# A layer of attention and RWKV-7: softmax exponentials placed further behind their scores in a hand-made plan

## The chip, the core and the metric

The kernel runs on one core of one Trainium2 chip. The metric is device time in microseconds. Five engines matter: PE (TensorE, the matrix engine), DVE (VectorE), ACT (ScalarE), POOL (GpSimd) and SP (SyncE, which issues DMAs). Each works through its own queue in order; a tile passes from one to another through semaphores.

## What is computed

One decoder layer over 2048 tokens of width 1024, in float32. After an RMS norm, one projection feeds two groups of heads side by side: eight attention heads with two key-value heads, and eight RWKV-7 heads. Their outputs share one output projection; then come a gated feed-forward part with a causal convolution and a last RMS norm. The change touches the attention heads alone. Cut to what matters there:

```python
def sliding_window_attention(q, k, v, sinks):
    # per block of 128 queries: its own 128 keys and the 128 before them
    s = jnp.einsum('bnqkgd,bnskd->bnkgqs', qb, kb) * (HEAD_DIM ** -0.5)
    s = s - slopes[:, :, None, None] * dist.astype(f32)
    s = jnp.where(valid[None, :, None, None], s, NEG_INF)
    m = jnp.maximum(jnp.max(s, axis=-1, keepdims=True), sink)
    p = jnp.exp(s - m)
    denom = jnp.sum(p, axis=-1, keepdims=True) + jnp.exp(sink - m)
    o = jnp.einsum('bnkgqs,bnskd->bnqkgd', p / denom, vb)
```

The RWKV-7 heads run a recurrence over the tokens, `S_t = S_(t-1) (diag(w_t) - kk_t^T (a_t kk_t)) + v_t^T k_t`, `y_t = S_t r_t`; the kernel computes it in chunks.

## The kernel before

**Two stages.** Up to about 1212 us the kernel projects, attends and runs the recurrence; after that come the rest of the output projection and the feed-forward part, which the change doesn't touch. The first stage is cut into 16 units: four blocks `b` of 512 tokens by four pairs `j` of heads. A unit (b, j) is named so below. The names of its tiles end in `_b_j_...`.

**What a unit holds.** Its backbone is a chain of eight chunks of the recurrence: PE products into `pc` and `pY`, and between them evictions by ACT: `Pt`, `Ut`, `SV`. Each chunk needs the one before, so between its products PE has gaps ("hops", 24 in a unit), which are filled with two kinds of work. The dense pieces are matmuls of the input projection for a later unit (`pin_q`, `pin_r`, ...). The placed pieces have a position from 0 to 24 in the unit, from the table `Q` at the top of the file (L43 to L80), and are issued when the chain has come so far. Among them are the attention of the unit before, the output of the recurrence (`py`, `pg`), a triangular substitution on DVE (`Mt`, `M`, 31 steps, one step woven in behind each other DVE instruction), and the loading and transposing of the next block's input (`ht`).

**The attention of a unit** comes in four quarters (q2, g): two halves of the block's queries, two key-value heads. A quarter has three placed pieces, with a row of four positions each in `Q["at0"]` to `Q["at3"]`, one table for each pair:

- scores (L1006): products into `pS` on PE; DVE adds the bias and takes the maximum (`P<-pS`), then writes the negated maximum and one more small operand, both into the tile `m`.
- transposes (`ptr`, L1054): PE transposes the normalised P into `pT`; ACT copies it rounded (`pth`), DVE takes the rest (`ptl`).
- value products (`pv`, L1070): twelve products into `pO`, evicted by ACT to `oT`.

`pS`, `pT` and `pO` share one PSUM pool with two buffers, the P tiles a pool with two as well.

**What is deferred.** Between scores and transposes lie two more steps. They are not placed by position: a planner's clock, which counts microseconds of planned work (L396 to L411), runs them later. `go1` (L1038) puts the exponentials of the sink and of the scores on ACT, due `Q["p1"]` after the scores. `go2` (L1045) adds the sums, takes the reciprocal and normalises P, all on DVE, due `Q["p2"]` after `go1`. If they are still to do when the transposes are issued, `need` runs them first:

```python
def tick(us):
    clk["t"] += us
    while todo and todo[0][0] <= clk["t"]:
        todo.pop(0)[2]()
```

All of PE, ACT and DVE are issued through `in_order` (L94), which ties each instruction to the one before it on its engine. So the plan is the order of the queues: an instruction whose operand is late holds all that stand behind it on its engine.

Of the kernel before, what the change touches and what calls it, by code (L numbers as in the profile page):

```python
# [54 lines left out]
    "y2": 1.5,  # L55
    "ql": 1.0,
    "p2": 1.2,
    "p1": 1.8,
    "tl": 0.8,
    "hop": 0.25,  # L60
    "sub": (6.5, 17.0, 21.0, 22.0, 23),
# [1787 lines left out]
```

## Time and profile before

| | |
|---|---|
| median of three runs | 2682.79 us (2681.02 to 2684.7) |
| profiled execution | 2685.55 us |
| its span | 2683.8 us |
| PE busy | 2534.4 us, 94% of the span |
| DVE, ACT, POOL busy | 1740.1, 1285.3, 1469.0 us |

The profiled execution is 2.76 us over the median. Busy time of PE is an upper view, since matmuls are pipelined and their ends are modelled. An instruction's row in the timeline gives its start, its length, engine and line, what it writes and reads, and in brackets how long the engine stood idle before it and which instruction on which engine released it.

### The profile page before, as it was taken

What the parts mean: (1) busy time and instruction counts of PE and PEld (TensorE: products, weight loads), DVE (VectorE), ACT (ScalarE), POOL (GpSimd) and SP (SyncE); (2) the same over time, 40 slices, a digit from 0 to 9 for tenths busy, and PEclk for the clock granted to TensorE, in tenths of its full rate; (3) what the DMA queues carried; (4) which work ended last, traced back from release to release, by engine and by line L of the source; (5) the groups of instructions that cost most, each with busy time, mean ns of one, the idle gap of its engine ahead of it and who ended that gap; (6) DMA issues with size and microseconds to landing.
All of it is one profiled execution on the core that took longest, in us unless ns stands there. A gap on an engine that the chain in (4) does not pass through costs nothing.

```text
span 2683.8 us, 42227 instructions
## 1 busy us (share of the span) xinstructions
PE 2534.4 (94%) x15211; PEld 1988.0 (74%) x15211; DVE 1740.1 (65%) x3232; ACT 1285.3 (48%) x2753; POOL 1469.0 (55%) x1364
## 2 busy tenths in 40 slices
PE   7799999999999989998989999999999999999997
PEld 5566766767667666776768788787888888888886
DVE  6568776777677757644756777867676765453336
ACT  4356655665556555543434434345343343343343
POOL 6334443444444434321637777777666665564598
PEclk9899998999999989899979999999999999999999
DMA  4222222222223222335662444545233326742354
GB/s 126 62 70 74 74 71 74 66 68 76 70 59 96 64 66 74 80 116 182 189 203 86 157 141 144 161 162 192 83 110 102 118 91 233 237 158 102 102 166 172
DMA packets 333108, 313.94 MB, mean 117 GB/s; under 512 B 102576, under 2 KB 254274, under 8 KB 332898
## 3 DMA queue, kind: packets, MB, share of 16 engines
q1 hardware_dynamic: 332290, 310.71, 38.1%
q8 instruction: 119, 1.95, 0.3%
q14 instruction: 91, 0.75, 0.1%
q10 hardware_dynamic: 608, 0.53, 0.1%
HBM read 229.26 MB, written 81.92 MB: 116 GB/s over the span
## 4 chain that ended last, share of the span: by engine, by line
PE 62%; DVE 17%; DMA 7%; ACT 5%; issue 4%; POOL 4%; SPq 0%; POOLq 0%; ACTq 0%; DVEq 0%
PE q_g L104 14%; PE d L104 14%; PE q_u L104 13%; DVE M L124 4%; DVE Mt L124 4%; PE pin_q L104 3%; PE poa L104 3%; DMA LL<-dL 3%; PE px L104 2%; PE po L104 2%; PE pc L104 2%; DVE P L124 2%; PE pin_k L104 1%; PE ph L104 1%; PE pO L104 1%
## 5 line engine op out<-in xcount | busy, mean ns | idle before, releaser
L1262 POOL TENSOR_TENSOR ul_u<-s_u,uh_u 128x512 fp32r<-128x512 f32 x154 | 214.4, 1401 | 138.0 <-ACT uh_u L110 134.8
L1262 POOL TENSOR_TENSOR ul_a<-sa,uh_a 128x512 fp32r<-128x512 f32 x154 | 210.9, 1377 | 139.7 <-ACT uh_a L110 139.7
L1262 POOL TENSOR_TENSOR ul_g<-s_g,uh_g 128x512 fp32r<-128x512 f32 x154 | 220.9, 1442 | 60.9 <-ACT uh_g L110 54.8
L104 PE MATMUL q_g<-h2h,uh_g 128*128 128x512 f32 x616 | 242.6, 394 | 10.0 <-DVE u_g L1486 5.9
L104 PE MATMUL q_g<-h2l,uh_g 128*128 128x512 f32 x616 | 241.7, 392 | 0.0
L104 PE MATMUL q_g<-h2h,ul_g 128*128 128x512 f32 x616 | 241.5, 393 | 0.1
L104 PE MATMUL q_u<-h2h,uh_u 128*128 128x512 f32 x616 | 240.2, 390 | 1.3 <-DVE ct L1486 1.0
L104 PE MATMUL q_u<-h2h,ul_u 128*128 128x512 f32 x616 | 239.9, 389 | 0.9 <-POOL ul_u L1262 0.9
L104 PE MATMUL q_u<-h2l,uh_u 128*128 128x512 f32 x616 | 239.7, 389 | 0.0
L104 PE MATMUL d<-ul_b,uh_a 128*128 128x512 f32 x616 | 232.9, 390 | 1.8 <-DVE ul_b L1483 1.8
L104 PE MATMUL d<-uh_b,ul_a 128*128 128x512 f32 x616 | 229.5, 389 | 0.0
L110 ACT ACTIVATE uh_a<-sa 128x512 fp32r<-128x512 f32 x154 | 97.1, 631 | 229.1 <-PE d L104 122.3
L104 PE MATMUL d<-uh_b,uh_a 128*128 128x512 f32 x616 | 205.9, 389 | 0.0
L110 ACT ACTIVATE uh_u<-s_u 128x512 fp32r<-128x512 f32 x154 | 95.1, 628 | 223.5 <-DVE s_u L1483 113.8
L124 DVE TENSOR_TENSOR Mt<-M,LL 128x60 f32<-128x60 f32 (+24 forms) x496 | 159.2, 321 | 41.7 <-DMA LL<-dL 33.3
L110 ACT ACTIVATE uh_g<-s_g 128x512 fp32r<-128x512 f32 x154 | 95.3, 629 | 186.3 <-PE q_u L104 102.7
L1483 DVE TENSOR_TENSOR ul_b<-wd,uh_b 128x512 fp32r<-128x512 f32 x55 | 68.6, 1249 | 156.1 <-ACT uh_b L110 150.1
L124 DVE SCALAR_TENSOR_TENSOR cc<-g,fcst,cc 128x1024 f32<-128x1024 f32 x88 | 145.4, 1670 | 29.1 <-ACT cc L110 28.4
L124 DVE TENSOR_TENSOR M<-M,Mt 128x60 f32<-128x60 f32 (+24 forms) x496 | 155.7, 314 | 10.8
L104 PEld LDWEIGHTS q_g<-h2h,uh_g 128*128 128x128 f32 x616 | 117.0, 190 | 36.0 <-DVE u_g L1486 7.2
L104 PEld LDWEIGHTS d<-ul_b,uh_a 128*128 128x128 f32 x616 | 115.6, 188 | 27.8 <-DVE ul_b L1483 4.1
L104 PEld LDWEIGHTS q_u<-h2h,uh_u 128*128 128x128 f32 x616 | 115.6, 188 | 27.2 <-DVE ct L1486 1.4
(371 smaller groups left out, 7017.5 us busy)
## 6 DMA issues: line engine op xcount, KB each, us to landing
sa<-actc SPq DMA_DIRECT2D x77, 512.0 KB
s_g<-in_ffn_w_gate_dram SPq DMA_DIRECT2D x44, 512.0 KB
s_u<-in_ffn_w_up_dram SPq DMA_DIRECT2D x44, 512.0 KB
actc<-cc SPq DMA_DIRECT2D x88, 256.0 KB
actc<-sa SPq DMA_DIRECT2D x66, 256.0 KB
wd<-in_ffn_w_down_dram SPq DMA_DIRECT2D x22, 512.0 KB
s_cat<-catT SPq DMA_DIRECT2D x20, 512.0 KB
x<-in_x_dram SPq DMA_DIRECT2D x16, 512.0 KB
```

The costliest lines, as they stand in the source:

```text
L104: in_order("pe", nc.tensor.matmul(**kw))
L110: in_order("act", nc.scalar.activation(*args, **kw))
L124: in_order("dve", f(*args, **kw))
L1262: return nc.gpsimd.tensor_tensor(out=out, in0=in0, in1=in1, op=ALU.subtract)
L1483: return nc.vector.tensor_tensor(out=out, in0=in0, in1=in1, op=ALU.subtract)
```

## The change

Two entries of the table change; no instruction is added or removed.

```diff
--- before.py
+++ after.py
@@ -55,7 +55,7 @@
     "y2": 1.5,
     "ql": 1.0,
     "p2": 1.2,
-    "p1": 1.8,
+    "p1": 4.0,
     "tl": 0.8,
     "hop": 0.25,
     "sub": (6.5, 17.0, 21.0, 22.0, 23),
@@ -69,7 +69,7 @@
     "py": (10, 10, 11),
     "vt": 1,
     "xl": (4, 14, 16, 23.6),
-    "at0": ((6.5, 9, 17.5, 18.5), (9.5, 13.5, 20, 20.0), (13, 16, 20.5, 22)),
+    "at0": ((6.5, 9, 16.5, 18.0), (10.5, 13.5, 20, 21.5), (13, 16, 21, 23)),
     "at1": ((4.5, 6, 13.5, 15.5), (8, 12.5, 18.5, 21.5), (10, 17.5, 20.5, 23)),
     "at2": ((4.5, 6, 13.5, 17.0), (9, 13, 18, 21), (11.0, 14, 20, 23)),
     "at3": ((4, 6, 10, 14), (8.5, 11.5, 16.5, 19.5), (10.5, 13.5, 19.5, 23.6)),
```

`p1` puts the exponentials, and with them the normalisation, later behind their scores by the planner's clock: 4.0 us in place of 1.8. It holds for all units. In `at0`, the table of the first pair of each block, the third and fourth scores come earlier (17.5 to 16.5, 18.5 to 18.0), the first and fourth transposes later (9.5 to 10.5, 20.0 to 21.5), and so do the third and fourth value products (20.5 to 21, 22 to 23).

In the built program PE's order changes in the four units of pair 0 alone. On ACT and DVE the exponentials and normalisations of all pairs move.

Unit (1, 1), ACT: `m` and `P` are the exponentials of the third quarter, `Pt` and `Ut` the evictions of chunk 5, `sh_v3` and `carry` belong to the input of a later unit. Before:

```order
L110 ACTIVATE SV_1_1_4512<-pc_1_1_4_5800,eC2_134 64x64 x2
L110 ACTIVATE m_1_1_1_0_5856<-m_1_1_1_0_5856 128x2
L110 ACTIVATE P_1_1_1_0_5855,m_1_1_1_0_5856<-P_1_1_1_0_5855,m_1_1_1_0_5856 128x256 x2
L110 ACTIVATE Pt_1_1_5_5898<-pc_1_1_5_5897 128x64
L110 ACTIVATE sh_v3_1_5958<-pin_v3_1_5793,omu_118 128x512
L110 ACTIVATE carry_119<-pin_v3_1_5793 128x1
L110 ACTIVATE Ut_1_1_5_5899<-pc_1_1_5_5897 128x64
```

After:

```order
L110 ACTIVATE SV_1_1_4512<-pc_1_1_4_5800,eC2_134 64x64 x2
L110 ACTIVATE Pt_1_1_5_5895<-pc_1_1_5_5894 128x64
L110 ACTIVATE m_1_1_1_0_5856<-m_1_1_1_0_5856 128x2
L110 ACTIVATE P_1_1_1_0_5855,m_1_1_1_0_5856<-P_1_1_1_0_5855,m_1_1_1_0_5856 128x256 x2
L110 ACTIVATE sh_v3_1_5950<-pin_v3_1_5793,omu_118 128x512
L110 ACTIVATE carry_119<-pin_v3_1_5793 128x1
L110 ACTIVATE Ut_1_1_5_5896<-pc_1_1_5_5894 128x64
```

The first eviction of the chunk now stands ahead of the exponentials.

The same unit, DVE: the last steps of the substitution (`M`, `Mt`) with the normalisation of the third quarter (`m` twice, `P` twice) between them; `hr` and `v` are pieces of later inputs. Before:

```order
L124 RECIPROCAL m_1_1_1_0_5856<-m_1_1_1_0_5856 128x2
L124 TENSOR_TENSOR Mt_1_2_30_5946<-M_1_2_5491,LL_1_2_5490 128x8
L124 TENSOR_SCALAR P_1_1_1_0_5855<-P_1_1_1_0_5855,m_1_1_1_0_5856 128x256
L124 TENSOR_TENSOR M_1_2_5491<-M_1_2_5491,Mt_1_2_30_5946 128x8
L124 TENSOR_SCALAR P_1_1_1_0_5855<-P_1_1_1_0_5855,m_1_1_1_0_5856 128x256
L124 TENSOR_TENSOR hr_2_2_3351<-pth_11_1_5967,cst0_107 128x2x128
L124 TENSOR_TENSOR hr_2_3_3352<-pth_11_1_5967,cst0_107 128x2x128
L124 SCALAR_TENSOR_TENSOR v_1_3_5957<-pin_v3_1_5793,cst1_108,sh_v3_1_5958 128x511
L124 SCALAR_TENSOR_TENSOR v_1_3_5957<-carry_119,cst1_108,sh_v3_1_5958 128x1
L124 TENSOR_TENSOR m_1_1_1_1_5914<-m_1_1_1_1_5914 128x2
```

After:

```order
L124 TENSOR_TENSOR hr_2_2_3348<-pth_11_1_5956,cst0_107 128x2x128
L124 TENSOR_TENSOR M_1_2_5491<-M_1_2_5491,Mt_1_2_29_5933 128x8x2
L124 TENSOR_TENSOR hr_2_3_3349<-pth_11_1_5956,cst0_107 128x2x128
L124 TENSOR_TENSOR Mt_1_2_30_5964<-M_1_2_5491,LL_1_2_5490 128x8
L124 SCALAR_TENSOR_TENSOR v_1_3_5949<-pin_v3_1_5793,cst1_108,sh_v3_1_5950 128x511
L124 TENSOR_TENSOR M_1_2_5491<-M_1_2_5491,Mt_1_2_30_5964 128x8
L124 SCALAR_TENSOR_TENSOR v_1_3_5949<-carry_119,cst1_108,sh_v3_1_5950 128x1
L124 TENSOR_TENSOR m_1_1_1_0_5856<-m_1_1_1_0_5856 128x2
L124 RECIPROCAL m_1_1_1_0_5856<-m_1_1_1_0_5856 128x2
L124 TENSOR_SCALAR P_1_1_1_0_5855<-P_1_1_1_0_5855,m_1_1_1_0_5856 128x256 x2
```

The normalisation now stands behind two `hr` and two `v`.

Unit (1, 0), PE, near its end: `pT_1_0_1_1` are the fourth transposes, `pO_1_0_1_0` the third value products, `pc_1_0_7` the products of the last chunk, `pin_q1` the dense work. Before:

```order
L104 MATMUL pin_q1_1_5212<-hh_1_3_2702,wh_q1_1_5062 128x512
L104 MATMUL pin_q1_1_5212<-hl_1_3_2703,wh_q1_1_5062 128x512
L104 MATMUL pin_q1_1_5212<-hh_1_3_2702,wl_q1_1_5063 128x512
L107 MATMUL pT_1_0_1_1_5244<-ident_64,P_1_0_1_1_5156 128x128 x4
L104 MATMUL pO_1_0_1_0_5252<-pth_1_0_1_0_5230,vth_130 64x128
L104 MATMUL pO_1_0_1_0_5252<-ptl_1_0_1_0_5231,vth_130 64x128
L104 MATMUL pO_1_0_1_0_5252<-pth_1_0_1_0_5230,vtl_131 64x128
```

After:

```order
L104 MATMUL pO_1_0_1_0_5256<-pth_1_0_1_0_5226,vth_130 64x128
L104 MATMUL pO_1_0_1_0_5256<-ptl_1_0_1_0_5227,vth_130 64x128
L104 MATMUL pO_1_0_1_0_5256<-pth_1_0_1_0_5226,vtl_131 64x128
L107 MATMUL pT_1_0_1_1_5272<-ident_64,P_1_0_1_1_5153 128x128 x4
L104 MATMUL pc_1_0_7_5244<-Pt_1_0_7_5245,TT0_139 64x64 x2
L104 MATMUL pin_q1_1_5208<-hh_1_4_2736,wh_q1_1_5062 128x512
L104 MATMUL pin_q1_1_5208<-hl_1_4_2737,wh_q1_1_5062 128x512
```

The fourth transposes stood ahead of the twelve third value products; they now stand behind them, and behind the first products of chunk 7, which come ahead of those.

Unit (0, 0), PE: `pT_0_0_0_0` are the first transposes, `pw_0_2` a projection of RWKV, `pc_0_0_3` the products of chunk 3. Before:

```order
L104 MATMUL pw_0_2_1432<-wah_0_411,lwh_114 128x512
L104 MATMUL pw_0_2_1432<-wal_0_412,lwh_114 128x512
L104 MATMUL pw_0_2_1432<-wah_0_411,lwl_115 128x512
L107 MATMUL pT_0_0_0_0_1441<-ident_64,P_0_0_0_0_1324 128x128 x3
L104 MATMUL pc_0_0_3_1397<-Pt_0_0_3_1398,TT0_139 64x64 x2
L104 MATMUL pin_r2_0_1467<-hh_0_0_205,wh_r2_0_1273 128x512
L104 MATMUL pin_r2_0_1467<-hl_0_0_213,wh_r2_0_1273 128x512
```

After:

```order
L104 MATMUL pw_0_2_1438<-wah_0_411,lwh_114 128x512
L104 MATMUL pw_0_2_1438<-wal_0_412,lwh_114 128x512
L104 MATMUL pw_0_2_1438<-wah_0_411,lwl_115 128x512
L104 MATMUL pc_0_0_3_1390<-Pt_0_0_3_1391,TT0_139 64x64 x2
L107 MATMUL pT_0_0_0_0_1450<-ident_64,P_0_0_0_0_1324 128x128 x3
L104 MATMUL pin_r2_0_1464<-hh_0_0_205,wh_r2_0_1273 128x512
L104 MATMUL pin_r2_0_1464<-hl_0_0_213,wh_r2_0_1273 128x512
```

The transposes here move behind one pair of products. In the units (1, 0), (2, 0) and (3, 0) they move behind 24 to 30 rows, among them twelve matmuls of `pin_r2`.

## Rows read from the trace of the kernel before

**Rows 1.** Windows: us; busy (instructions) PE, PEld, DVE, ACT, POOL; PEclk, DMA, GB/s
```profile
421.00:697.00 276.00, 256.94 (x2153) 190.89 (x2152) 201.45 (x563) 166.79 (x438) 118.75 (x144) 0.96 0.27 70
```

**Rows 2.** List of waits, 145 to 1212 us: total us, times, longest
```profile
ACT m L110 <- DVE m L124: 79.1, 35, 5.4
...
PE pT L107 <- DVE P L124: 21.5, 19, 3.7
PE pc L104 <- ACT Pt L110: 17.4, 18, 2.8
...
DVE P L124 <- PE pS L104: 57.1, 25, 7.6
```

**Rows 3.** Timeline of PE: start, length, instruction, [idle before it and its releaser]
```profile
181.90 0.33 PE L104 MATMUL pc<-Ut,Bt 64*64 64x64 f32 x4 [1.08 <-ACT Ut L110]
...
1076.42 0.33 PE L104 MATMUL pc<-Ut,Bt 64*64 64x64 f32 x4 [0.77 <-ACT Ut L110]
```

**Rows 4.** Timeline of ACT, block 1, pair 1
```profile
516.48 0.20 ACT L110 ACTIVATE m<-m 128x2 f32<-128x2 f32 x1 [5.31 <-DVE m L124]
```

**Rows 5.** Timeline of PE, block 1, pair 1
```profile
517.97 0.33 PE L104 MATMUL pc<-Pt,TT 64*64 64x64 f32 x4 [2.78 <-ACT Pt L110]
...
524.35 0.34 PE L104 MATMUL pc<-SV,W 128*64 128x64 f32 x4
...
524.85 0.66 PE L107 MATMUL pT<-ident,P 128*128 128x128 f32 x4
```

**Rows 6.** Timeline of DVE, block 1, pair 1
```profile
523.90 0.35 DVE L124 TENSOR_SCALAR P<-P,m 128x256 f32<-128x256 f32 x1
524.16 0.75 DVE L124 TENSOR_TENSOR hr<-pth,cst 128x256 f32<-128x256 f32 x2
524.83 0.74 DVE L124 SCALAR_TENSOR_TENSOR v<-pin_v,cst,sh_v 128x511 f32<-128x511 f32 x1
525.48 0.21 DVE L124 SCALAR_TENSOR_TENSOR v<-carry,cst,sh_v 128x1 f32<-128x1 f32 x1
```

**Rows 7.** One DVE row, the POOL row beside it, and the DVE row's group
```profile
520.75 1.26 DVE L124 TENSOR_TENSOR M<-M,Mt 128x24 f32<-128x24 f32 x1
...
520.70 1.27 POOL L132 TENSOR_TENSOR BK<-BK,sw 128x512 f32<-128x512 f32 x1 [6.71 <-DVE BK L124]
...
L124 DVE TENSOR_TENSOR M<-M,Mt 128x60 f32<-128x60 f32 (+24 forms) x496 | 155.7, 314 | 10.8
```

**Rows 8.** Window behind 517.97: us, PE busy (instructions), PEclk, DMA, GB/s
```profile
519.30:522.80 3.50, 3.50 (x26) 0.52 0.46 150
```

**Rows 9.** Timeline of PE, block 1, pair 3
```profile
663.51 0.78 PE L107 MATMUL pT<-ident,P 128*128 128x128 f32 x4 [0.60 <-DVE P L124]
```

**Rows 10.** Timeline of DVE, block 1, pair 3
```profile
663.71 0.74 DVE L124 SCALAR_TENSOR_TENSOR v<-pin_v,cst,sh_v 128x511 f32<-128x511 f32 x1
...
664.50 0.68 DVE L124 TENSOR_TENSOR ptl<-pT,pth 128x512 fp32r<-128x512 f32 x1
```

**Rows 11.** Timeline of PE, block 1, pair 2
```profile
578.08 0.33 PE L104 MATMUL pc<-Pt,TT 64*64 64x64 f32 x4 [1.78 <-ACT Pt L110]
```

**Rows 12.** Timeline of PE, block 1, pair 0: fourth transposes, third value products
```profile
462.07 0.44 PE L107 MATMUL pT<-ident,P 128*128 128x128 f32 x2 [1.56 <-DVE P L124]
...
463.94 0.28 PE L104 MATMUL pO<-pth,vth 128*64 128x128 f32 x1 [0.16 <-DVE ptl L124]
...
464.65 0.22 PE L104 MATMUL pO<-pth,vtl 128*64 128x128 f32 x1
```

**Rows 13.** Timeline of DVE, block 1, pair 0: the bonus product
```profile
443.13 0.69 DVE L124 TENSOR_TENSOR bv<-pb,v 128x512 f32<-128x512 f32 x1 [3.10 <-PE pb L104]
```

**Rows 14.** Timeline of DVE, then of PE, block 0, pair 0
```profile
152.93 0.28 DVE L124 TENSOR_SCALAR P<-P,m 128x128 f32<-128x128 f32 x1
...
157.48 0.22 DVE L124 TENSOR_TENSOR Mt<-M,LL 128x60 f32<-128x60 f32 x1
...
154.59 0.48 PE L104 MATMUL pc<-Pt,TT 64*64 64x64 f32 x4 [0.51 <-ACT Pt L110]
```

## The prediction

> **What bounds the kernel now.** I read the windows first, for where the engines differ by stage. In one block of the first stage [rows 1] PE is busy 257 of 276 us and VectorE (DVE) 201, so PE has 19 us of holes per block, and only holes can be won or lost: no instruction is added or removed. What follows after 1212 us is untouched. The list of waits [rows 2] then says who makes the holes. PE waits 21.5 us for normalised probabilities P (from DVE) and 17.4 us for Pt, the first eviction of a recurrence chunk (from ScalarE, ACT). ACT itself stands 79.1 us in front of exponentials whose negated maximum m DVE has not written yet. Since ACT works in order, every eviction behind such an exponential stands too. The timeline of PE shows what that costs: eleven waits of PE, up to 2.8 us, come directly after such a stall and sum to 17.3 us; [rows 3] are the first and the last. That is the prize the change reaches for.
>
> The unit of block 1, pair 1 shows the mechanism and its limit. ACT stands 5.31 us at the exponential [rows 4]; Pt comes behind it and PE waits 2.78 us for it [rows 5]. But 6.9 us later PE starts the third transposes at 524.85, and the P that they read was normalised by 523.90 + 0.35 = 524.25 [rows 6]: 0.60 us of margin. DVE runs without a hole over this half of the unit. So the Pt wait is not on the path by itself: were it gone, PE would come earlier and wait at the transposes for the same P. What counts is when DVE finishes P.
>
> **The change part by part** (times against the profiled execution, 2685.55 us).
>
> *Exponential behind the evictions, pair 1.* ACT now makes Pt first, so the 2.78 us wait goes. But the normalisation falls back in DVE's queue too, behind two products hr and two pieces of v: from 524.16 to 525.48 + 0.13 (the pitch to the next row) = 1.45 us of DVE work [rows 6]. P ends at 525.70, 0.85 us after the transposes start now. PE has nothing else in its order, so it stands there: +0.85 us for the unit. The work jumped is not lost, but DVE reaches the fourth P at the same time as before, and PE needs that only two slots later. Block 2's unit has the same rows (+0.85); in block 0's PE waits already, without margin (+1.4); block 3's falls behind v alone (+0.79, the pitch from 663.71 to 664.50 in [rows 10]). Sum **+3.9 us**; ends 0 (DVE arrives earlier by its margin) and 5.1 (no margin anywhere).
>
> *The same, pair 3.* Here P already makes PE wait 0.60 us [rows 9]. The fourth normalisation falls behind v and one ptl: from 663.71 to 664.50 + 0.60 = 1.39 us [rows 10]. No margin, so twice 1.4 (blocks 0 and 1) and 1.5 in block 2, which by the order passes the same kind of work: **+4.3 us**; ends 0 and 6.
>
> *The same, pair 2.* The normalisation falls behind 1.5 us of work as well, but right before those transposes PE waits 1.78 us for a Pt [rows 11] that ACT delays for an operand of DVE's own. That wait is set by DVE, and covers the later P: **0**; if the cover is gone, +2.
>
> *Pair 0, fourth transposes.* Before, PE waits 1.56 us there for P [rows 12] with twelve value products (463.94 to 464.65, pitch 0.065: 0.78 us) and the three products of the next chunk still to do (0.50 us, from 524.35 to 524.85 in [rows 5], full clock). The change puts both ahead of the transposes, into the wait. So after P comes 1.28 us less is left, in four blocks: **−5.1 us**. The last value products move to the end of the unit, and cost there what they cost before. The ends are −5.1 and 0: the oT eviction also shifts, and a two-buffer PSUM pool is shared by scores, transposes and products, so a tile freed later could hold PE at the next.
>
> *Pair 0, first transposes, block 0.* Here the transposes move behind one pair of products only, but their normalisation moves from 152.93 to behind the substitution row at 157.48 [rows 14]. PE's next dense matmul follows the Pt products, so it moves from 154.59 + 0.33 = 154.9 to about 157.7 + 0.5 = 158.2: +3.3 us. The third transposes there fall behind v, +0.8. Sum **+4.1**, ends 0 (by the third pair DVE is ahead again) and 6.6 (twice the 3.3).
>
> *Pair 0, first transposes, blocks 1 to 3.* These go behind 24 to 30 rows of PE work, over 5 us, so PE should meet P finished. DVE gains only where it waits for PE: 3.10 us at the bonus product in block 1 [rows 13], a shorter one in block 3. Up to −4.3; I take **−2**, as the third scores also come earlier and the delayed exponentials share the DVE stretch behind it.
>
> *The clock.* After a wait of PE the granted clock drops: behind the 2.78 us wait it was 0.52 for 3.50 us, with PE full [rows 8]; 0.52 is the lower of the two levels, 1.2 GHz. Such a stretch does 3.5 × 0.48 = 1.7 us less. Before, it lay ahead of the transposes, where PE had to wait for P anyway. After, the wait is at the transposes, and the slow stretch behind them has no cover. Six units (pair 1 and pair 3 of three blocks): 0 to 10 us; I take half, **+5.1**.
>
> *ScalarE, SyncE, GpSimd.* ACT has idle time (191 to 201 us are PEld and DVE, ACT 167 of 276 in [rows 1]), so its later exponentials only matter through P. Transfers on SP's queue and GpSimd's halves of the weight split shift by a row: 0; if an LL transfer came later, DVE would start its substitution later by as much.
>
> Sum: 3.9 + 4.3 + 0 − 5.1 + 4.1 − 2 + 5.1 = **+10.3 us**, 2696 us for the profiled execution. That execution is 2.8 us over the median of the three runs, 2682.79; carried over, 2682.8 + 10.3 = **2693 us**.
>
> One rule of the Trainium skill speaks to the size of the delay. A DVE row of substitution took 1.26 us where rows of its group take 0.314 on average; a GpSimd product ran beside it [rows 7]. "GPSIMD Engine Reference", § 1. Specifications, says that the two engines share their SBUF interfaces and contend when a DVE instruction has two SBUF inputs or a 2-port mode; the trace agrees. By it, moving normalisations among other GpSimd work could add 0.95 us to each of the six that decide, an estimate of +5.7 to the sum, or take as much off. The forecast does without it.
>
> **The rivals.**
>
> *R1, the freed ACT pays (faster).* The evictions come earlier, so the recurrence and with it the scores and PSUM tiles come earlier; DVE, which waits 57.1 us for scores in this stage [rows 2], starts its half of each unit earlier, and P is not later at all. It decides where DVE gains over 0.85 us per unit before the normalisations. In full it gives −17.3 (the eleven waits) −5.1 = −22, that is 2660; half of the units −11, 2672. For it: the 57.1 us. Against: in the halves shown DVE has no hole, and its order is fixed. "Perfetto Trace Analysis", § Optimization Strategy, of the Trainium skill would have it so: find the gaps of the binding engine and have what they wait for start sooner; [rows 3] are such gaps.
>
> *R2, waits only change place.* Every wait of PE for Pt turns into one for P of the same length, the lost and the won in pair 0 cancel, the clock is as often down as before. Then 0 ± 5: 2683. For it: the substitution and vector work of a unit is the same sum in both orders.
>
> *R3, worse.* No gain in pair 0 (the 7.1 us of its two negative terms are not won) and all six slow stretches uncovered (+5.1 more): 10.3 + 7.1 + 5.1 = +22, 2705.
>
> That the change does nothing is excluded by the order of the built program: the exponentials and normalisations of 63 of 64 quarters move.
>
> **How the numbers follow.** A difference of 0.2% (5.4 us) is about what a measurement of this kernel can tell from none. Forecast 2693: 0.42; R1 0.26; R2 0.22; R3 0.10. Faster by over 0.2% is R1: 0.27. Within: R2, 0.23. Slower: forecast and R3, 0.50. The range takes half of R1 (2670) and most of R3 (2705); about 1 in 10 is left at each side. The ends of all terms at once are 9 us under the time before and 30 over it; that they fall to one side together is unlikely, and the forecast alone stands for some 2685 to 2702.
>
> **What the profile after would show.** Right: PE's waits for Pt fall from 17.4 us towards 10, its waits for P rise from 21.5 to over 30, the longest (4 to 5 us) at block 0's first and at the third and fourth transposes of pairs 1 and 3, each followed by some us at a granted clock near 0.5. DVE's 3.10 us at the bonus product is gone; the fourth transposes of pair 0 still wait, briefly. Wrong: waits for P no higher, with DVE's waits for scores falling (R1); or a new releaser ahead of pT, such as a PSUM tile or ptl, in pair 0 (R3).

## The result and the profile after

The changed kernel takes 2714.42 us (median of four runs, 2706.13 to 2720.03) against 2683.74 us (four runs beside it): ratio 1.0099, 95% interval 1.0074 to 1.0124, so some 27 us slower. The forecast was 2693 us, slower by 10, with a range up to 2705. The sign was right; the size was not, and the range was too narrow above. The profiled execution of the changed kernel (2720.03 us, span 2718.3) ends its first stage 33.6 us later than that of before (1244.3 against 1210.8 us), and the rest takes 1474 us as against 1473. Nearly all of the loss lies where the change is. That execution is the slowest of the four, 5.6 us over their median, so its sums run a little high.

The table of windows over the first stage (us; PE busy and its instructions; granted clock; DMA share; GB/s), the kernel before and then the changed one:

```profile
130.00:1212.00 1082.00, 1011.50 (x8512) 0.97 0.29 75
```

```profile
130.00:1245.60 1115.60, 1024.56 (x8510) 0.94 0.28 72
```

The same PE work (two records fewer) takes 33.6 us more. Of these PE is idle 20.5 us more (91.0 against 70.5), and busy 13.1 us more with the same instructions: that goes with the granted clock, 0.94 on average in place of 0.97. (Over whole executions it was 0.964 to 0.970 in the four of the changed kernel, and 0.965 to 0.978, median 0.970, in the 31 of the kernel before that ran beside e9 to e12.)

The list of waits of the changed kernel over the same stretch (total us, times, longest), which answers to [rows 2]:

```profile
PE pT L107 <- DVE P L124: 68.2, 27, 6.5
...
PE pc L104 <- ACT Ut L110: 3.3, 6, 1.0
PE pc L104 <- ACT Pt L110: 2.8, 5, 0.8
...
ACT m L110 <- DVE m L124: 14.6, 10, 3.1
...
DVE P L124 <- PE pS L104: 67.2, 23, 10.6
```

What the change reached for, it reached. ACT's stand in front of exponentials fell from 79.1 to 14.6 us, PE's waits for Pt from 17.4 to 2.8 and for Ut from 10.3 to 3.3; the line for Ut before was

```profile
PE pc L104 <- ACT Ut L110: 10.3, 13, 1.9
```

But PE's waits for P rose from 21.5 to 68.2 us. DVE's waits for scores, which R1 wanted to fall, rose from 57.1 to 67.2.

I cut the first stage into its 16 units, from the first `pc` product of one to that of the next in PE's timeline, and summed by pair what each took more than before (us). "Busy" is what is left when PE's idle time is taken away; with equal work it is clock, apart from a few rows that cross a unit's border.

| | length | idle | busy | waits for P | waits for Pt and Ut |
|---|---|---|---|---|---|
| pair 0 | +4.0 | +8.0 | −4.0 | +13.2 | −4.9 |
| pair 1 | +21.7 | +14.5 | +7.2 | +18.8 | −7.6 |
| pair 2 | +12.9 | +1.0 | +11.9 | +6.4 | −5.8 |
| pair 3 | −5.3 | −2.7 | −2.6 | +8.4 | −3.3 |

In these two profiles pair 1 and pair 2 make the loss, in two ways: pair 1 mostly by idle time, pair 2 by clock. Each row is the difference of one execution to one other. In runs that leave a pair's code as it was, its sum still moved by up to 9 us (pair 0 by −5.1 in e3 and −4.5 in e9, pair 3 by +4.6 in e9, pair 2 by +8.7 in e2), so the figures of pairs 0 and 3 are no larger than that spread, and pair 2's not by much. (The first expectations below quote other sums by pair, −1.3, 25.2, 13.3 and −3.6. They were cut at the end of the recurrence chain; since the new table moves products across that point, the cut above is the fairer one.)

The unit that the prediction took as its pattern, block 1, pair 1, in PE's timeline after (answers to [rows 5]):

```profile
527.99 0.33 PE L104 MATMUL pc<-Pt,TT 64*64 64x64 f32 x4
...
539.14 0.90 PE L107 MATMUL pT<-ident,P 128*128 128x128 f32 x3 [4.58 <-DVE P L124]
```

The Pt products no longer wait; the third transposes stand 4.58 us for P. Before, the one waited 2.78 us and the other started without a wait.

### The profile page after: what moved, and what is told of

Same layout as the page of the kernel before. It is cut to its first block, busy times and chain, and to the rows that moved or that the text cites. A ratio compares the mean times of both kernels' runs of the same rounds, so it can differ in the third digit from the quotient of the medians.

```text
span 2718.3 us, 42240 instructions
## 1 busy us (share of the span) xinstructions
PE 2542.1 (94%) x15211; PEld 1996.7 (73%) x15211; DVE 1738.8 (64%) x3232; ACT 1285.4 (47%) x2753; POOL 1475.0 (54%) x1364
## 4 chain that ended last, share of the span: by engine, by line
PE 44%; DVE 3%; POOL 3%; DMA 3%; issue 2%; ACT 1%; SPq 0%; POOLq 0%; DVEq 0%; ACTq 0%
PE d L104 13%; PE q_g L104 13%; PE q_u L104 13%; PE poa L104 2%; PE po L104 2%; POOL ul_a L1262 1%; DMA s_g<-in_ffn_w_gate_dram 1%; DMA xt<-in_x_dram 1%; DMA swo<-in_w_out_dram 1%; DMA s_u<-in_ffn_w_up_dram 1%; POOL ul_u L1262 0%; POOL rso L1752 0%; POOL ul_g L1262 0%; PE pc L104 0%; DVE xn L124 0%
## 5 line engine op out<-in xcount | busy, mean ns | idle before, releaser
L124 DVE TENSOR_TENSOR Mt<-M,LL 128x60 f32<-128x60 f32 (+24 forms) x496 | 148.7, 300 | 51.3 <-DMA LL<-dL 42.8
L124 DVE TENSOR_TENSOR M<-M,Mt 128x60 f32<-128x60 f32 (+24 forms) x496 | 171.8, 346 | 10.4
L104 PEld LDWEIGHTS d<-ul_b,uh_a 128*128 128x128 f32 x616 | 115.6, 188 | 27.7 <-DVE ul_b L1483 3.9
```

Of the source, the lines that this page charges most:

```text
L104: in_order("pe", nc.tensor.matmul(**kw))
L124: in_order("dve", f(*args, **kw))
```

## The experiments

They ran in three batches (e1 to e4, e5 to e8, e9 to e12), each on a chip of its own. The ratio is to the kernel before, run beside each batch on the same chip; medians of different batches compare only through it. "Stage" is how much later than before the first stage ends in the profiled execution; waits are PE's, in us.

| run | what it is | median us | ratio (95%) | stage | for P | for Pt |
|---|---|---|---|---|---|---|
| | changed kernel | 2714.4 | 1.0099 (1.0074–1.0124) | +33.6 | 68.2 | 2.8 |
| e1 | p1 alone | 2727.5 | 1.0172 (1.0150–1.0193) | +41.6 | 78.1 | 2.8 |
| e2 | table alone | 2690.0 | 1.0007 (0.9983–1.0031) | +10.9 | 8.7 | 23.1 |
| e3 | p1 in pair 1 alone | 2708.5 | 1.0106 (1.0075–1.0137) | +7.4 | 38.2 | 8.3 |
| e4 | changed, PE filled in pair 1 | 2698.4 | 1.0050 (1.0028–1.0073) | +12.5 | 53.0 | 2.8 |
| e5 | table, p1 in pairs 2 and 3 | 2688.9 | 0.9998 (0.9979–1.0017) | −0.8 | 21.8 | 19.2 |
| e6 | table, normalisation late, exponentials not | 2708.4 | 1.0068 (1.0046–1.0091) | +30.6 | 39.4 | 22.5 |
| e7 | table, exponentials late, normalisation not | 2700.4 | 1.0038 (1.0013–1.0063) | +10.5 | 17.7 | 13.6 |
| e8 | changed, PE filled at four places | 2699.3 | 1.0038 (1.0018–1.0059) | +11.4 | 29.9 | 3.0 |
| e9 | before, PE filled at pair 2's start | 2683.6 | 0.9970 (0.9946–0.9993) | −0.8 | 22.2 | 16.5 |
| e10 | table, filled as e9 | 2688.6 | 1.0000 (0.9976–1.0024) | +6.4 | 8.0 | 25.2 |
| e11 | changed, filled as e9 | 2703.3 | 1.0044 (1.0021–1.0067) | +18.9 | 67.4 | 3.0 |
| e12 | table, p1 in pair 3, filled as e9 | 2684.3 | 0.9971 (0.9953–0.9988) | −1.3 | 16.8 | 21.5 |

Executions of one kernel differ by over 1%: the kernel before took 2674.65 to 2709.79 us over 31 runs. So I go by ratios and by the rows, and by medians only where both agree.

### Which part loses: e1, e2, e3

```diff
e1  -    "p1": 1.8,
    +    "p1": 4.0,
e2       (the new "at0" alone)
e3  -                    defer(Q["p1"], go1, f"p_{u}")
    +                    defer(4.0 if j == 1 else Q["p1"], go1, f"p_{u}")
```

> p1 = 4.0 alone, the table of pair 0 as before. By units, the profile of the changed kernel puts its 33.6 us of loss at -1.3 us in the four units of pair 0, +25.2 in pair 1, +13.3 in pair 2 and -3.6 in pair 3, so theory A is that p1 alone makes the loss: +30 to +42 us over the kernel before, waits of PE for P again near 68 us. Theory B, that pair 0's later transposes and p1 make it only together, has under +15 us and waits for P under 40 us.

> The table of pair 0 alone, p1 = 1.8 as before. Theory A: a small gain, by my term for the fourth transposes -5 us (ends -7 and 0), with PE's waits for P falling from 21.5 us to some 12. Theory B: pair 0's new places are themselves harmful, +8 us or more.

> p1 = 4.0 in the four units of pair 1 alone, all else as before. If the cause lies where the loss shows (pair 1, and the slow-clock stretches after it in pair 2): +15 to +30 us, waits of 3.8 to 4.6 us at the third transposes of pair 1. If the loss is spread over all pairs and only shows there: some +8 us (a quarter).

p1 alone loses 1.7%, more than the whole change: theory A holds, and the new table wins part of it back. By units (cut as above) p1 alone costs 23.3 us in pair 0, where the old places of the transposes meet the late P; with the new table that is 4.0. The table alone is within 0.3% of the kernel before; the gain of 5 us that I expected isn't seen. Its profile shows 7.0 us less in pair 0, with the waits for P there down from 16.1 to 2.3 us, and a loss at the clock elsewhere. But only 2.1 of the 7.0 us are idle time, and pair 0 moved by −4.5 and −5.1 us in e9 and e3 with the old table, so a gain from the table isn't shown. e2's waits:

```profile
PE pc L104 <- ACT Pt L110: 23.1, 16, 4.2
...
PE pT L107 <- DVE P L124: 8.7, 8, 2.3
PE pO L104 <- DVE ptl L124: 6.8, 3, 2.5
```

Waits for P fell to 8.7 us (I had expected some 12), but waits for Pt rose by 5.7 and for ptl by 5.9. e3 lost 1.1% at the median. Its profiled execution was its fastest (2697.4 us, 11 under the median), and even that has 14.5 us more in pair 1, of which 12.0 idle. With p1 late in its units alone pair 1 costs as much as the whole change; its third transposes wait 17.8 us there.

### Whose order: e6, e7

Both keep the new table. e6 keeps the order of ACT and PE of the run with the table alone, row by row, and moves only the normalisation on DVE. e7 leaves the normalisation due where it was and moves the exponentials, though by 1.2 us and not by 2.2; in pair 1 its order on DVE and PE is that of the table alone.

```diff
e6  -    "p2": 1.2,  "p1": 4.0,
    +    "p2": 3.4,  "p1": 1.8,
e7  -    "p2": 1.2,  "p1": 4.0,
    +    "p2": 0.0,  "p1": 3.0,
```

> The new table, with p1 = 1.8 and p2 = 3.4: ACT's order is that of the run with the new table alone, row by row, while the normalisation is due 5.2 us behind the scores, as in the changed kernel. If the late normalisation on DVE makes the loss: slower than before by +25 us or more, waits of PE for P 55 us or more, and waits for Pt still near 17 to 23. If the new order on ACT makes it: within 8 us of the kernel before, waits for P under 25 us.

> The new table, with p1 = 3.0 and p2 = 0: the normalisation is due 3.0 us behind the scores, as before the change, and the exponentials go 1.2 us later than before, 56 of 64 behind at least one more row of ACT. If DVE's order makes the loss, this has none: waits for P under 20 us, waits for Pt under 12, and the time 2 to 10 us under the run with the new table alone. If ACT's order makes it, or DVE now stands for the exponentials instead: +10 us or more over the kernel before, with DVE's waits for P from ACT up by as much.

e6 in the lists of waits and the table of windows:

```profile
PE pT L107 <- DVE P L124: 39.4, 25, 3.5
PE pc L104 <- ACT Pt L110: 22.5, 13, 4.1
...
ACT m L110 <- DVE m L124: 79.6, 39, 5.9
...
130.00:1242.60 1112.60, 1028.66 (x8509) 0.94 0.28 73
```

Here ACT stands 79.6 us in front of exponentials as ever, PE waits 22.5 us for Pt, and the stage still ends 30.6 us late in the profile, almost as in the changed kernel. That execution is the slowest of six, 11 us over their median; by the ratio the loss is 0.7%, two thirds of the change's (1.0%), with intervals that overlap. I had expected +25 us, which is more than the ratio gives (+18), and waits for P of 55 us or more, where they are 39.4. The changed kernel waits 28.8 us more for P than e6 and 22.1 us less for Pt and Ut (6.1 against 28.2): with ACT's evictions freed, most of these waits turn into waits for P. So, by the ratios, the late normalisation alone makes some two thirds of the loss, and the freed evictions win nothing that shows.

e7 shows the other side:

```profile
PE pT L107 <- DVE P L124: 17.7, 9, 2.9
PE pc L104 <- ACT Pt L110: 13.6, 15, 2.4
...
DVE m L124 <- ACT P L110: 34.2, 22, 3.3
```

Waits for P came out as expected (under 20 us), for Pt a little above the 12 that I gave. But the run is 0.4% slower, not faster: DVE now stands 34.2 us in front of its own normalisation (7.5 before), for exponentials that ACT makes later. The rival got this part right. Most of it falls in pair 1, which takes 14.4 us more than before in this profile (8.0 of it idle), where the table alone has +4.5 (1.5 idle) and e6 +18.6 (10.2 idle). In its block 1 DVE takes 10.32 us from the first maximum of the third quarter to the end of its P, as against 9.30 in e2, though its rows there keep their order: one more of them, of 1.21 us, runs beside a GpSimd product. So in pair 1 either step costs when it alone comes later. Both finish P later; DVE's order alone is not the cause.

### What the clock adds: e4, e8, e11

e4 and e8 put matmuls on data at hand ahead of transposes, where PE stands for P; what they write is overwritten by the transposes. e11 puts four ahead of the first `pY` products of each pair-2 unit, into a tile that nothing reads, and leaves the waits for P as they are.

```diff
e4  +  if j == 1 and q2 == 1 and g == 0:
    +      for _ in range(16):
    +          mm(out=pT..., lhsT=vth[:, 1], rhs=vth[:, 1:5]..., start=True, stop=True)
e8  +  nfill = {(0, 0, 0): 10, (0, 1, 0): 7, (1, 1, 0): 16, (3, 1, 1): 9}.get((j, q2, g), 0)
e11 +  if j == 2:                       # chunk 0, ahead of y1(pY=pY)
    +      for _ in range(4):
    +          mm(out=pF, lhsT=kTh[:, 0, 1], rhs=kTh[:, 0, 1:5]..., start=True, stop=True)
```

> The changed kernel with sixteen more 128x512 matmuls on data at hand (about 3.7 us of PE at full clock) put ahead of the third transposes in the four units of pair 1, where PE stands 3.8 to 4.6 us for P; their result is overwritten. If the clock that falls after these waits is a cost of its own: 8 to 15 us faster than the changed kernel, though PE has more work, with the slow stretches behind them gone. If only the wait for P counts: within 3 us of it. If the added matmuls delay something else: slower by up to 15 us.

> The changed kernel with added matmuls ahead of four transposes of a unit where PE stands for P: 10 ahead of pair 0's first, 7 ahead of its third, 16 ahead of pair 1's third, 9 ahead of pair 3's fourth (0.23 us each). With pair 1's alone the time fell from 2714 to 2698 us. If the clock is a cost at each such wait: 2685 to 2693 us. If pair 1's were the only ones that mattered: 2696 to 2702. If the additions now exceed the waits: slower than 2702.

> The changed kernel with the same four matmuls at the start of pair 2 only; the waits for P are left as they are. Its profile lost 13.3 us in pair 2, some 20 us of PE at the low clock in three stretches. If these begin at the place that is filled: 2700 to 2707 us in place of 2714. If they are the aftermath of the waits for P in pair 1: 2711 to 2718.

With 64 matmuls more, e4 is 16 us faster than the changed kernel by the medians and 13 by the ratios (1.0050 against 1.0099). In its profile the stage is 21 us shorter than in that of the changed kernel: 8.9 us in pair 1, 13.9 in pair 2. Pair 2 was not touched; there the clock stayed up in three of its four units, whether by the filling or by chance isn't shown. The first 20 us of the unit of block 1, pair 2 in the changed kernel, with its first rows on PE, and the same stretch before, with the same two rows, and in e4 (its second row is e4's whole stage):

```profile
556.94 2.05 PE L104 MATMUL px<-W,BK 64*128 64x128 f32 x16 [0.20 <-DVE W L124]
559.90 0.48 PE L104 MATMUL pY<-SV,W 128*64 128x64 f32 x4 [0.91 <-ACT ysq L110]
```

```profile
556.30:576.30 20.00, 18.89 (x100) 0.58 0.23 45
```

```profile
541.10 2.05 PE L104 MATMUL px<-W,BK 64*128 64x128 f32 x16 [0.20 <-DVE W L124]
544.05 0.34 PE L104 MATMUL pY<-SV,W 128*64 128x64 f32 x4 [0.91 <-ACT ysq L110]
...
540.40:560.40 20.00, 18.50 (x155) 1.00 0.29 60
```

```profile
546.40:566.40 20.00, 18.51 (x156) 1.00 0.28 61
...
130.00:1224.50 1094.50, 1018.18 (x8568) 0.97 0.29 74
```

In the changed kernel PE is as busy there as before (18.89 against 18.50 of 20 us) but does 100 instructions in place of 155, at a granted clock of 0.58 on average: most of the stretch ran at the lower level, 1.2 GHz. The drop follows 2 us of 64-row `px` products and a wait of 0.91 us for ACT. That wait is in every kernel that doesn't fill it, and the clock falls behind it in some units and not in others: before in one block of four (for 14 us), in the changed kernel in all four, for 3 to 17 us. e11 fills just that wait:

```profile
554.28 2.05 PE L104 MATMUL px<-W,BK 64*128 64x128 f32 x16 [0.23 <-DVE W L124]
556.26 1.19 PE L104 MATMUL pF<-kTh 128*128 128x512 f32 x4
557.39 0.34 PE L104 MATMUL pY<-SV,W 128*64 128x64 f32 x4
...
553.40:573.40 20.00, 19.48 (x161) 1.00 0.28 53
```

The clock holds at 1.00, pair 2 falls from +12.9 to −3.1 us, and the median to 2703, inside what I had given; pair 1 keeps its +21.2 us and the waits for P their 67.4. So two costs can be told apart: the waits for P, and a place at the start of pair 2 where the clock may fall. How much of the second belongs to the change is less sure. Filling the place takes 0.55% off the changed kernel and 0.30% off the kernel before, and with it filled in both (e11 and e9, on one chip) the change still costs 20 us by the medians. Over whole executions e11's granted clock is that of the kernel before (median 0.970 in both), and e11 is still 0.44% slower. Why the clock falls there in one unit and not in another is open. Late P alone doesn't decide it: in e2, where PE hardly waits for P, it fell in three of four units (pair 2 +8.7 us), in e5 in all four (+7.0), in e4, with 53.0 us of waits for P, in one.

e8 filled more and won nothing beyond e4 that shows (1.0038 against 1.0050, with intervals that overlap); I had given 2685 to 2693 us if the clock were a cost at each wait. The clock was up (0.98 over the stage), but PE was busy 1040.7 us in place of the 1011.5 of the kernel before. So filling the other three places won back no more than its own matmuls cost.

### Which pairs pay, and what can be had: e5, e9, e10, e12

```diff
e5  +  defer(Q["p1"] if j > 1 else 1.8, go1, f"p_{u}")      (changed kernel)
e9     (the kernel before, with the four matmuls of e11)
e10    (the new table alone, with them)
e12 +  defer(4.0 if j == 3 else Q["p1"], go1, f"p_{u}")     (e10)
```

> The new table of pair 0 with p1 = 4.0 in pairs 2 and 3 alone and 1.8 in pairs 0 and 1. If the loss belongs to pairs 0 and 1, where a unit's third or first transposes wait longest: within 5 us of the run with the new table alone, 2685 to 2695 us, with some 5 to 8 us more of waits for P in pairs 2 and 3. If every pair pays for p1: +8 us or more over that run.

> The kernel before with four 128x512 matmuls on data at hand (0.9 us), thrown away, ahead of the first pY products of each pair-2 unit, where PE waits 0.91 us after its 64-row px products. In the profiles the long slow-clock stretches begin there (three of four units in the changed kernel, one of four before). If that place decides whether the clock falls: no stretch at the start of pair 2, and 0 to 8 us under the kernel before. If the stretches come from elsewhere: same time, stretches still there.

> The new table of pair 0 alone, with the same four matmuls at the start of pair 2. Alone the table won 7.8 us in pair 0 in its profile and lost 8.4 in pair 2 to the clock. If the filling holds the clock: 2674 to 2682 us, faster than the kernel before. If not: 2685 to 2692.

> The new table, p1 = 4.0 in pair 3 alone, and the four matmuls at the start of pair 2: what won or cost nothing in the runs so far. By the units of the earlier profiles the late exponentials of pair 3 change -1 to -4 us. If they add to the run with table and filling: 2672 to 2680 us. If the wait for P in pair 3 costs as much as it frees: within 3 us of that run.

e5: the late exponentials of pairs 2 and 3 cost nothing (0.9998, as against 1.0007 in e2), though PE waits 13 us more for P than in e2. e9 and e12 are 0.3% under the kernel before, with intervals that end just below 1; of twelve runs that is weak evidence. e10 did not show what I expected of it (2674 to 2682 us): it took 2688.6. Its four matmuls held the clock at pair 2's start, but in its profile the clock fell elsewhere (pair 3: +9.8 us, all busy). In the profiles of e9 to e12 no drop at the start of pair 2 is left in any of the 16 units. That the table or the late pair 3 adds to the filling is not shown: e12 and e9 are level, and e12 missed the 2672 to 2680 us that I had given.

## Why the prediction was right or wrong

**The bound and the mechanism** were right in the main. PE waits for P, and the freed waits for Pt and Ut (27.7 us before, 6.1 after) did not pay: the changed kernel itself shows both. That DVE's queue decides when P is ready is shown by e6; e7 adds that late exponentials can hold DVE as well, for which the sum had no term. Rival R1 (17.3 us to be had) fell: its waits went, and the kernel became slower. R2, waits that only change place, fell too: P takes 4.58 us where Pt took 2.78. R3 came nearest in time, but its sign, a PSUM tile or ptl ahead of pT in pair 0, did not come. By "Perfetto Trace Analysis", § Optimization Strategy, of the Trainium skill the gaps of the binding engine were to be closed. They were, and others opened beside them: PE's waits for P rose from 21.5 to 68.2 us.

**Pair 1, +3.9 us and its part of the clock: the mis-sized term.** It measured +21.7, 14.5 of it idle. I had DVE rows jumped (1.45 us) and a margin of 0.60. From DVE's first maximum of the third quarter to the end of its P it took 9.28 us in blocks 1 and 2 before, and 11.50 after: 2.22 more, not 1.45, so 1.62 us beyond the margin, where I had 0.85. Rows on DVE after (answers to [rows 6, 7]), with one on GpSimd:

```profile
532.20 1.03 DVE L124 TENSOR_TENSOR M<-M,Mt 128x35 f32<-128x35 f32 x1
...
534.46 1.25 DVE L124 TENSOR_TENSOR M<-M,Mt 128x24 f32<-128x24 f32 x1
...
536.18 0.97 DVE L124 TENSOR_TENSOR M<-M,Mt 128x16 f32<-128x16 f32 x1
...
538.73 0.61 DVE L124 TENSOR_SCALAR P<-P,m 128x256 f32<-128x256 f32 x2
...
531.88 1.30 POOL L132 TENSOR_TENSOR wl_q<-w_q,wh_q 128x512 fp32r<-128x512 f32 x1 [5.02 <-ACT wh_q L110]
```

The same DVE row before, `M<-M,Mt` of 35 columns:

```profile
519.32 0.19 DVE L124 TENSOR_TENSOR M<-M,Mt 128x35 f32<-128x35 f32 x1
```

It took 0.19 us then and 1.03 now. A GpSimd product (`wl_q`, 531.88 to 533.18) runs beside it that met other work before, and the DVE row ends 0.05 us after it. In the stretch to P there are three such long rows now (those at 532.20, 534.46 and 536.18), two before; each ends within 0.05 us of the end of a GpSimd product. Taken together these rows cost DVE 0.6 us more than before: with the 1.45 that is 2.05 of the 2.22. In block 0 there are five in place of three. The prediction had this beside its sum: "GPSIMD Engine Reference", § 1. Specifications, of the Trainium skill says that DVE and GpSimd share their SBUF interfaces, and the estimate by it was 0.95 us for each P that decides. The trace agrees: 0.84 in this row. In the sum it should have stood, for rows that move on DVE also move against GpSimd. But this, 0.8 us in a unit beyond what I had, is the smaller part of the miss. In block 1 the unit took 3.8 us more: 1.80 at the third transposes (4.58 for P in place of 2.78 for Pt), 1.04 at a product that waits for Ut, 0.45 at one that waits for W, which the table alone has too, and a small rest. Blocks 0 and 3 lost 6.6 us each, with a second stretch at the low clock behind a second wait (1.26 us for ptl, 4.40 for P at the first transposes); the sum had neither. Why those two waits came I have not traced.

**Pair 0, blocks 1 to 3, first transposes: wrong.** I wrote that PE should meet P finished behind 24 to 30 rows of its own work. It stood there for 2.72, 4.01 and 6.47 us (rows 2 to 4; the first is block 0):

```profile
158.27 0.89 PE L107 MATMUL pT<-ident,P 128*128 128x128 f32 x2 [6.02 <-DVE P L124]
...
447.23 0.90 PE L107 MATMUL pT<-ident,P 128*128 128x128 f32 x3 [2.72 <-DVE P L124]
...
732.64 0.90 PE L107 MATMUL pT<-ident,P 128*128 128x128 f32 x3 [4.01 <-DVE P L124]
...
1020.35 0.90 PE L107 MATMUL pT<-ident,P 128*128 128x128 f32 x3 [6.47 <-DVE P L124]
```

The working counted PE's side and not how far the normalisation falls back on DVE. In block 1, from the exponentials to P:

```profile
438.93 0.51 ACT L110 ACTIVATE P<-P,m 128x256 f32<-128x256 f32 x1
...
446.83 0.35 DVE L124 TENSOR_SCALAR P<-P,m 128x256 f32<-128x256 f32 x1
447.24 0.35 DVE L124 TENSOR_SCALAR P<-P,m 128x256 f32<-128x256 f32 x1
```

From 438.93 to 447.59 it takes 8.66 us (2.54 before), with the opening of the substitution and the next maxima of scores ahead of it on DVE.

**Pair 0, the rest: right for the fourth transposes, one term missing.** The fourth transposes wait 1.2 us in place of 8.0 (I had −5.1). But the third wait 8.9 us in place of 1.8, and for them the sum had 0.8 us, in block 0 alone. That the table alone has 7.0 us less in pair 0, where my two terms sum to 7.1, is luck: 4.9 of the 7.0 are busy time. DVE's 3.10 us at the bonus product of block 1 is gone; block 3's is not (1.41). In block 0 the first transposes wait 6.02 us (I had about 4.5), and the unit costs 4.0 against my 4.1. The whole pair came to +4.0 in place of −3.0. The waits that the sum lacked are those of the first transposes in blocks 1 to 3 (13.2 us, 5.3 before) and of the third.

**Pair 3, +4.3: wrong, as the wait was covered.** The waits for P came, 8.4 us more, most of them at the quarter that I named (2.86 us in block 1, in place of 0.60). But PE waited for DVE further on in these units anyway, and those waits went: before, in the list of waits,

```profile
PE ph L104 <- DVE T L124: 3.7, 2, 2.0
...
PE pth L107 <- DVE bv L124: 3.0, 2, 1.5
```

After, neither is left. It is the cover that I saw for pair 2 and didn't look for in pair 3. e5 shows it as well: no loss with pairs 2 and 3 late. That the pair came out shorter (−5.3 us) is within the spread of single profiles.

**Pair 2, 0: right for the waits** (idle +1.0 us; the 6.4 us for P replace 5.8 for Pt and Ut), wrong in all, by 11.9 us of clock in this profile.

**The clock, +5.1 (0 to 10): too small and in the wrong place.** Measured +13.1 us. I counted one short stretch behind each new wait; these are there, but the longest (some 17 us in block 1) begin at the start of pair 2, behind no wait for P. The kernel before has the same weak place. In its profile the clock fell there in block 3 alone, to 0.51 from 1104 to 1117 us with PE full; I read only the short stretch of [rows 8], and took the chance of others at nothing.

By pair the miss is +7.0 (pair 0), +12.7 (pair 1, with all of the clock term set against it), +12.9 (pair 2) and −9.6 (pair 3). These sum to 23.0, the gap between +10.3 and the units' +33.4 within rounding. The steps that failed are thus the size of the delay in pair 1, P's time for the first and third transposes of pair 0, and the clock, whose chance to fall at a place with no wait for P the sum left out.

## What to carry to other kernels

A wait that goes away on one engine is worth only what the next one behind it leaves: look up who paces that, here DVE, and count what the move does to that engine's queue first. When a row moves behind others, add what those rows will meet on the engine that runs beside it, not just their mean length. And where the trace shows the granted clock falling at some place in one unit, look whether the other units have the same place, and put the chance that it falls there too into the range: here the clock made 13.1 us beside 20.5 us of waits.

## What the hardware showed that I had not expected

Work added to the engine that bounds the kernel made it faster. Sixteen useless matmuls in each of four waits took 16 us off the changed kernel (2714 to 2698; ratio 1.0099 to 1.0050). Four of them in each pair-2 unit, 0.9 us of PE time, took 11 us off (2703; ratio 1.0044), and in block 1's unit the next 20 us went at a granted clock of 1.00 in place of 0.58. On the kernel before they took 0.3% (ratio 0.9970, 0.9946 to 0.9993).
